# Attention with split key tiles: two float32r products for three, and one column of low parts summed beside TensorE

## The chip, the core and the metric

The kernel runs on one NeuronCore of a Trainium2 chip. The metric is the device time of one execution in microseconds. The kernel before took 1837.95 us in the median of three runs (1836.01 to 1842.63).

## The reference, cut to what matters

Two layers of a hybrid trunk (1152 tokens of width 1024: 128 context tokens, 1024 latent tokens). Each layer has one input projection, then four groups of heads side by side, then one output projection. Two of the groups are softmax attention and are what the change touches:

```
s = einsum('bqhgd,bkhd->bhgqk', qblk, k) * scale
p = softmax(s, axis=-1)
o = einsum('bhgqk,bkhd->bqhgd', p, v)          # float32 throughout
...
o_a = o_a * silu(ggate)                        # group A: 4 query heads on 2 key/value heads, dim 64
o_c = o_c * silu(mgate)                        # group C: 4 latent-attention heads, dim 96, values 64
o   = concat([o_a, o_b, o_c, o_d]) @ w_out
```

Context tokens read only the 128 context keys; latent tokens read 1280 keys (256 cached, 1024 latent). Groups B (gated linear attention) and D (a state-space scan) are chunked scans over the same tokens.

## The kernel before, in words

Everything is float32 in DRAM. Where TensorE multiplies in float32r, the operand is split into a high part (float32r) and a low part (value minus high part), and the product is the sum of the products of the parts; where it multiplies in plain float32, one instruction of the program leaves two matmul records in the trace.

Attention stands in `attend` (line 1093). There are 8 heads a layer, one after the other: four of group A, four of group C. A head has three query blocks (QBLK): block 0 with 128 queries and one key tile, blocks 1 and 2 with 512 queries and ten key tiles of 128 keys each. For one key tile j TensorE makes the scores transposed (keys on partitions, queries along the row) in a PSUM tile `st` (tag B, two buffers), by two (group A) or three (group C) float32r products (line 1102); ScalarE (ACT) takes their exponential; TensorE multiplies by the values into the PSUM tile `po` (tag C, one buffer), rows 0 to 63 the output, row 64 the sum of the weights (the values carry a column of ones).

The weights times values come in two kinds, by the number of the tile:

- even j: the exponential `P` stays float32, and one float32 product with `v` follows (lines 1117 and 1118);
- odd j ("split tiles"): ACT writes the exponential once as float32r (`Ph`, line 1107) and once more in place in float32 (line 1108), VectorE (DVE) subtracts (`Pl`, line 1110), and three float32r products follow: values high by Ph (1112), values low by Ph (1113), values high by Pl (1114). `v_parts` (1148) makes the parts of the values once a head.

At the end of a block ACT copies row 64 to `den` (1127) and rows 0 to 63 to `Ou` (1129); only then may the next block write `po`. For an odd head the sums go through DRAM and come back as reciprocals spread over 64 partitions (`R`), and GpSimd (POOL) multiplies them in (`gt`, line 1144), behind a DMA.

While attention runs, other work is in the same queues: the scans of groups B and D (lines 872 to 1061), for the next head the copies of queries and keys and a maximum over the scores (`maxima`, lines 755 and 756: a product on TensorE and a reduction on DVE), the splitting of the output weights (1085, 1086), and at the end the first tiles of the output projection. The order on each engine is not written out: a scheduler lays the program out in time by a model of its own and fixes each engine's queue; every engine then works its queue in order. So a change of one instruction moves others.

The kernel has one place already where ACT scales a tile by a column and POOL adds it to a sum, with one buffer between them (lines 173 and 174, in the modulation of the layers):

```
pr = wpool.tile([128, 512], F32, name="pr", tag="pr", bufs=1)
act.activation(out=pr, in_=st, func=AF.Identity, scale=c)
pool.tensor_tensor(out=acc[:, r, :], in0=acc[:, r, :], in1=pr, op=ALU.add)
```

Of the kernel before, what the change touches and what calls it, by code (L numbers as in the profile page):

```python
# [8 lines left out]
F32 = mybir.dt.float32  # L9
# [25 lines left out]
def hybrid_trunk_kernel(ctx: ExitStack, tc: tile.TileContext, a):  # L35
# [50 lines left out]
    mask = tri.bitcast(I32)  # L86
    gcum = const.tile([128, 2, 131], F32, name="gcum")
# [291 lines left out]
    for l in range(L):  # L379
# [466 lines left out]
        with ExitStack() as sta:  # L846
# [246 lines left out]
            def attend(h, spasses, scale, v, vi, vh, vl, gate_rows, kd, st):  # L1093

                for b, (q0, nq, kts) in enumerate(QBLK):
                    qs = slice(q0, q0 + nq)
                    po = psC("po")
                    for j, kt in enumerate(kts):
# [5 lines left out]
                        if j % 2:  # L1104

                            Ph = at.tile([128, 512], F32R, name="Ph", tag="Ph", bufs=3)
                            act.activation(out=Ph[:, 0:nq], in_=sp_[:, 0:nq], func=AF.Exp, scale=scale)  # L1107
                            anchors["act"] = act.activation(out=sp_[:, 0:nq], in_=sp_[:, 0:nq], func=AF.Exp, scale=scale)  # L1108
                            Pl = at.tile([128, 512], F32R, name="Pl", tag="Pl", bufs=2)
                            anchors["dve"] = dve.tensor_tensor(out=Pl[:, 0:nq], in0=sp_[:, 0:nq], in1=Ph[:, 0:nq], op=ALU.subtract)  # L1110
                            k = j // 2
                            pe.matmul(po[0:65, 0:nq], lhsT=vh[:, k, :], rhs=Ph[:, 0:nq], start=False, stop=False, skip_group_check=True)
                            pe.matmul(po[0:64, 0:nq], lhsT=vl[:, k, :], rhs=Ph[:, 0:nq], start=False, stop=False, skip_group_check=True)
                            pe.matmul(po[0:65, 0:nq], lhsT=vh[:, k, :], rhs=Pl[:, 0:nq], start=False, stop=last, skip_group_check=True)  # L1114
                        else:
                            P = at.tile([128, 512], F32, name="P", tag="P", bufs=5)
                            anchors["act"] = act.activation(out=P[:, 0:nq], in_=sp_[:, 0:nq], func=AF.Exp, scale=scale)  # L1117
                            pe.matmul(po[0:65, 0:nq], lhsT=v[:, kt, vi, :], rhs=P[:, 0:nq], start=(j == 0), stop=last,  # L1118
                                      skip_group_check=True)
# [6 lines left out]
                    den = nrm.tile([1, 512], F32, name="den", tag="den", bufs=1)  # L1126
# [21 lines left out]
            def v_parts(v, i):  # L1148

                vh = at.tile([128, 5, 65], F32R, name="vh", tag="vh", bufs=2)  # L1150
                vl = at.tile([128, 5, 64], F32R, name="vl", tag="vl", bufs=2)
                act.copy(vh, v[:, 2:KT:2, i, :])
                yield
                pool.tensor_tensor(out=vl, in0=v[:, 2:KT:2, i, 0:64], in1=vh[:, :, 0:64], op=ALU.subtract)
                yield
                return vh, vl

            def prep_mla(h):
# [3 lines left out]
                if h == 0:  # L1162
                    wu = at.tile([128, 512], F32, name="wu", tag="P", bufs=5)
# [63 lines left out]
            def run_mla(h):  # L1227
# [3 lines left out]
                vh, vl = yield from v_parts(state["vm"], i)  # L1231
                yield attend(h, [(KA[i][0:96], QB[i][0:96]), (KA[i], QA[i]), (KB[i], QB[i])], 96.0 ** -0.5, state["vm"], i, vh, vl,
# [248 lines left out]
```

## Time and profile before

| | |
|---|---|
| median of 3 runs | 1837.95 us |
| the profiled execution | 1836.28 us, of which 1834.5 us are the span of the trace |
| attention of layer 0, about | 423 to 870 us of the span |
| attention of layer 1, about | 1300 to 1745 us |
| key tiles of 128 keys by 512 queries | 320: 160 split, 160 in float32 |
| block ends with 512 queries | 32 (2 layers, 8 heads, 2 blocks) |

The span runs from the first to the last instruction. The rows of the trace that the working uses stand in a section below, in numbered groups. In them PE is TensorE's matmuls, PEld its weight loads, DVE VectorE, ACT ScalarE, POOL GpSimd. Matmuls overlap in the pipeline and their ends are modelled, so what one costs in a stream is read from the distance of starts and not from its duration.

### The profile page before, as it was taken

To read this page: it belongs to the slowest core of one execution; us is meant where nothing else is said; L and a number is where in the kernel's file an instruction comes from. 1 tells how busy PE (TensorE), PEld (TensorE's weight loads), DVE (VectorE), ACT (ScalarE), POOL (GpSimd) and SP (SyncE) were. 2 spreads that over 40 slices of the span, in tenths; PEclk is the share of its full clock that TensorE was granted. 3 is DMA by queue.
4 is the path that set the end of the run, shared out by engine and by line. 5 is a ranking of instruction groups with operands and counts; after the bars stand their busy time and mean duration, and the time that the engine had idled before them with its cause. 6 is when DMAs were issued, how large, how long until landed. Compare 5 with 4: busy or idle time off the path is not lost.

```text
span 1834.5 us, 25155 instructions
## 1 busy us (share of the span) xinstructions
PE 1718.5 (94%) x8200; PEld 1312.8 (72%) x8200; DVE 1177.2 (64%) x2297; ACT 859.9 (47%) x1907; POOL 729.2 (40%) x909
## 2 busy tenths in 40 slices
PE   8999998998998998999999999999999899899998
PEld 2787977896665666656887999889666666565676
DVE  5738887647877886772453447543776788678223
ACT  4634422434654765673442162132465467567322
POOL 3633149824343543330343323871434354333011
PEclk9999988999989999999999999999998999999999
DMA  8435353413323321142433333231442332114243
GB/s 296 138 117 156 113 168 103 129 63 119 115 77 85 90 79 47 41 144 86 138 129 104 102 94 91 60 102 37 122 116 76 81 88 83 50 36 149 87 137 115
DMA packets 179684, 190.99 MB, mean 104 GB/s; under 512 B 29406, under 2 KB 140720, under 8 KB 179552
## 3 DMA queue, kind: packets, MB, share of 16 engines
q1 hardware_dynamic: 174208, 179.11, 32.1%
q10 hardware_dynamic: 5344, 10.26, 1.7%
q8 instruction: 65, 1.06, 0.3%
q14 instruction: 67, 0.55, 0.1%
HBM read 141.00 MB, written 48.30 MB: 103 GB/s over the span
## 4 chain that ended last, share of the span: by engine, by line
PE 54%; DVE 17%; DMA 11%; POOL 7%; issue 5%; ACT 4%; SPq 1%; ACTq 0%; POOLq 0%; DVEq 0%
PE psP L267 19%; PE op L267 8%; PE st L1102 5%; PE po L1118 5%; DMA ast<-in_w_ada_dram 2%; PE mx L755 2%; DMA wst<-in_w_in_dram 2%; DVE mx L756 2%; DVE Pl L1110 2%; PE po L1114 1%; DVE acc L176 1%; DMA R<-d_rec 1%; POOL wlo L261 1%; DVE d_DT L1023 1%; PE go L931 1%
## 5 line engine op out<-in xcount | busy, mean ns | idle before, releaser
L756 DVE TENSOR_REDUCE mx<-mx 128x1 f32<-128x512 f32 (+2 forms) x400 | 224.6, 582 | 92.2 <-PE mx L755 90.6
L267 PE MATMUL psP<-whi,hh 128*128 128x512 f32 (+2 forms) x576 | 202.6, 363 | 6.1 <-DVE whi L257 3.7
L267 PE MATMUL psP<-wlo,hh 128*128 128x512 f32 (+2 forms) x576 | 202.8, 361 | 2.1 <-POOL wlo L261 1.9
L267 PE MATMUL psP<-whi,hl 128*128 128x512 f32 (+2 forms) x576 | 187.5, 359 | 0.1
L261 POOL TENSOR_TENSOR wlo<-wst,whi 128x512 fp32r<-128x512 f32 (+3 forms) x106 | 130.6, 1240 | 137.9 <-DVE whi L257 79.0
L267 PE MATMUL psP<-hh,whi 128*128 128x384 f32 x480 | 163.1, 340 | 4.7 <-DVE whi L257 3.8
L1102 PE MATMUL st<-QA,KA 128*128 128x512 f32 (+1 forms) x336 | 164.0, 488 | 0.6 <-DVE Pl L1110 0.4
L267 PE MATMUL psP<-hl,whi 128*128 128x384 f32 x480 | 160.2, 336 | 0.0
L267 PE MATMUL psP<-hh,wlo 128*128 128x384 f32 x480 | 155.0, 337 | 0.1
L1110 DVE TENSOR_TENSOR Pl<-st,Ph 128x512 fp32r<-128x512 f32 x160 | 109.7, 686 | 65.9 <-ACT st L1108 64.2
L1107 ACT ACTIVATE Ph<-st 128x512 fp32r<-128x512 f32 x160 | 95.5, 597 | 107.5 <-PE st L1102 99.1
L1117 ACT ACTIVATE P<-st 128x512 f32<-128x512 f32 (+1 forms) x176 | 99.8, 567 | 79.1 <-PE st L1102 67.1
L1102 PE MATMUL st<-QB,KB 66*128 66x512 f32 (+3 forms) x336 | 133.0, 401 | 0.0
L267 PEld LDWEIGHTS psP<-whi,hh 128*128 128x128 f32 x576 | 110.3, 193 | 20.3 <-DVE whi L257 5.2
L267 PEld LDWEIGHTS psP<-wlo,hh 128*128 128x128 f32 x576 | 110.4, 193 | 17.9 <-POOL wlo L261 5.3
L267 PEld LDWEIGHTS psP<-whi,hl 128*128 128x128 f32 x576 | 108.5, 192 | 12.4 <-DVE hl L226 0.3
L1102 PEld LDWEIGHTS st<-QA,KA 128*128 128x128 f32 x336 | 65.4, 195 | 49.8 <-issue 39.3
L267 PEld LDWEIGHTS psP<-hh,whi 128*128 128x128 f32 x480 | 90.1, 188 | 12.0 <-DVE whi L257 5.5
L1102 PE MATMUL st<-QB,KA 96*128 96x512 f32 (+1 forms) x168 | 93.2, 555 | 2.1 <-ACT P L1117 1.8
L1108 ACT ACTIVATE st<-st 128x512 f32<-128x512 f32 x160 | 94.8, 592 | 0.0
L1118 PE MATMUL po<-P,vm 128*65 128x512 f32 (+1 forms) x176 | 88.7, 586 | 5.9 <-ACT P L1117 3.4
L1144 POOL TENSOR_TENSOR gt<-gt,R 128x512 f32<-128x512 f32 (+1 forms) x24 | 26.6, 1106 | 166.0 <-DMA R<-d_rec 162.3
(369 smaller groups left out, 4325.2 us busy)
## 6 DMA issues: line engine op xcount, KB each, us to landing
ast<-in_w_ada_dram SPq DMA_DIRECT2D x96, 256.0 KB
wst<-in_w_in_dram SPq DMA_DIRECT2D x64, 256.0 KB
wost<-in_w_out_dram SPq DMA_DIRECT2D x16, 512.0 KB
d_xs<-d_xb SPq DMA_DIRECT2D x32, 192.0 KB
ot<-d_oT SPq DMA_DIRECT2D x18, 320.0 KB
d_tok<-vv SPq DMA_DIRECT2D x18, 256.0 KB
d_gt<-gg SPq DMA_DIRECT2D x24, 192.0 KB
g_qk<-d_qk SPq DMA_DIRECT2D x36, 128.0 KB
```

Of the source, the lines that this page charges most:

```text
L176: dve.scalar_tensor_tensor(out=acc[:, r, :], in0=st, scalar=c, in1=acc[:, r, :], op0=ALU.mult, op1=ALU.add)
L261: eng.tensor_tensor(out=lo[:, 0:n], in0=st[:, 0:n], in1=hi[:, 0:n], op=ALU.subtract)
L267: pe.matmul(p, lhsT=lt, rhs=rh, start=(first and i == 0), stop=(last and i == n - 1))
L755: pe.matmul(p[:, 0:n], lhsT=lt_m[:, s], rhs=rh_m[:, o:o + n], start=True, stop=True)
L756: dve.tensor_reduce(out=mx[:, t, i:i + 1], in_=p[:, 0:n], axis=AX.X, op=ALU.max)
L1102: anchors["pe"] = pe.matmul(sp_[:, 0:nq], lhsT=kx[:, ks], rhs=qx[:, qs], start=(i == 0), stop=(i == len(spasses) - 1))
L1107: act.activation(out=Ph[:, 0:nq], in_=sp_[:, 0:nq], func=AF.Exp, scale=scale)
L1108: anchors["act"] = act.activation(out=sp_[:, 0:nq], in_=sp_[:, 0:nq], func=AF.Exp, scale=scale)
L1110: anchors["dve"] = dve.tensor_tensor(out=Pl[:, 0:nq], in0=sp_[:, 0:nq], in1=Ph[:, 0:nq], op=ALU.subtract)
L1117: anchors["act"] = act.activation(out=P[:, 0:nq], in_=sp_[:, 0:nq], func=AF.Exp, scale=scale)
L1118: pe.matmul(po[0:65, 0:nq], lhsT=v[:, kt, vi, :], rhs=P[:, 0:nq], start=(j == 0), stop=last, skip_group_check=True)
L1144: pool.tensor_tensor(out=g[:, 0:nq], in0=g[:, 0:nq], in1=R[:, 0:nq], op=ALU.mult)
```

## The change

In blocks 1 and 2 the split tiles are now the even ones (j = 0, 2, 4, 6, 8), so a block begins with a split tile and ends with a float32 one; block 0 has a float32 tile, as before. A split tile has two products instead of three: `vs` holds in one 128-column operand the high parts of the 64 values and the column of ones (columns 0 to 64) and the low parts of values 1 to 63 (columns 65 to 127). The first product, by Ph, uses all 128 columns, the second, by Pl, the first 65. What has no room is the low part of value 0 (`v0`): ACT multiplies Ph by that column (`acc` for the first split tile, `T0` for the four others), POOL adds the T0 to `acc` (the fourth addition goes to `accr` in float32r), and when the block ends one product with a column of ones (`oner`) adds the sum over the keys to row 0 of `po`.

At the end of a block ACT copies rows 64 to 127 of `po` (the sum of the weights and the low parts) to `lo`, and DVE adds them to rows 0 to 63 into `Ou`, with row 0 of `lo` masked by the column `nz`; so DVE's instruction takes the place of ACT's second copy. P has four buffers instead of five; T0, acc, accr and lo have one each.

```
-                        if j % 2:
+                        if b and j % 2 == 0:
...
                             k = j // 2
-                            pe.matmul(po[0:65, 0:nq], lhsT=vh[:, k, :], rhs=Ph[:, 0:nq], start=False, stop=False, skip_group_check=True)
-                            pe.matmul(po[0:64, 0:nq], lhsT=vl[:, k, :], rhs=Ph[:, 0:nq], start=False, stop=False, skip_group_check=True)
-                            pe.matmul(po[0:65, 0:nq], lhsT=vh[:, k, :], rhs=Pl[:, 0:nq], start=False, stop=last, skip_group_check=True)
+                            c = v0[:, k:k + 1]
+                            if k == 0:
+                                acc = at.tile([128, 512], F32, name="acc", tag="acc", bufs=1)
+                                act.activation(out=acc, in_=Ph, func=AF.Identity, scale=c)
+                            else:
+                                T0 = at.tile([128, 512], F32, name="T0", tag="T0", bufs=1)
+                                act.activation(out=T0, in_=Ph, func=AF.Identity, scale=c)
+                                to = acc if k < 4 else at.tile([128, 512], F32R, name="accr", tag="accr", bufs=1)
+                                anchors["pool"] = pool.tensor_tensor(out=to, in0=acc, in1=T0, op=ALU.add)
+                            pe.matmul(po, lhsT=vs[:, k, :], rhs=Ph, start=(j == 0), stop=False, skip_group_check=True)
+                            pe.matmul(po[0:65, :], lhsT=vs[:, k, 0:65], rhs=Pl, start=False, stop=False, skip_group_check=True)
...
+                    if b:
+                        pe.matmul(po[0:1, :], lhsT=oner, rhs=to, start=False, stop=True, skip_group_check=True)
...
-                    act.copy(den[:, 0:nq], po[64:65, 0:nq])
-                    sp.dma_start(out=d_den[kd, i, qs], in_=den[:, 0:nq])
-                    act.copy(O[64 * i:64 * i + 64, 0:nq], po[0:64, 0:nq])
+                    act.copy(lo[64 * i:64 * i + n, 0:nq], po[64:64 + n, 0:nq])
+                    sp.dma_start(out=d_den[kd, i, qs], in_=lo[64 * i:64 * i + 1, 0:nq])
+                    if b:
+                        dve.scalar_tensor_tensor(out=O[r, :], in0=lo[r, :], scalar=nz[r, :], in1=po[0:64, :], op0=ALU.mult, op1=ALU.add)
+                    else:
+                        act.copy(O[r, 0:nq], po[0:64, 0:nq])
...
-                vh = at.tile([128, 5, 65], F32R, name="vh", tag="vh", bufs=2)
-                vl = at.tile([128, 5, 64], F32R, name="vl", tag="vl", bufs=2)
-                act.copy(vh, v[:, 2:KT:2, i, :])
+                vs = at.tile([128, 5, 128], F32R, name="vs", tag="vs", bufs=2)
+                v0 = at.tile([128, 5], F32, name="v0", tag="v0", bufs=2)
+                x = v[:, 1:KT:2, i, :]
+                act.copy(vs[:, :, 0:65], x)
```

What the scheduler makes of it is shown at three places. First TensorE in layer 0, at the end of a 512-query block of head 5: `st` are scores of the next block, `mx` and `mT` belong to the maximum for the next head. Before:

```order
L1118 MATMUL po<-P,vm 65x512
L1102 MATMUL st<-QB_4250,KA_4247 128x128
L1102 MATMUL st<-QA_4249,KA_4247 128x128
L1102 MATMUL st<-QB_4250,KB_4248 128x128
L772 MATMUL mT<-identr,m 2x128 x4
L755 MATMUL mx<-KA_4247,QB_4250 128x512
L1112 MATMUL po<-Ph,vh 65x512
L1113 MATMUL po<-Ph,vl 64x512
L1114 MATMUL po<-Pl,vh 65x512
```

After:

```order
L1128 MATMUL po<-Ph,vs 128x512
L1129 MATMUL po<-Pl,vs 65x512
L1108 MATMUL st<-QB_4256,KA_4253 128x128
L1108 MATMUL st<-QA_4255,KA_4253 128x128
L1108 MATMUL st<-QB_4256,KB_4254 128x128
L778 MATMUL mT<-identr,m 2x128 x4
L761 MATMUL mx<-KA_4253,QB_4256 128x512
L1133 MATMUL po<-P,vm 65x512
L1138 MATMUL po<-accr,oner 1x512
```

The split tile's products moved to the front of the stretch, and the block is closed by the product with `oner`, which waits for POOL. Second ACT in layer 0, at the seam of heads 6 and 7 (`woh`, `wohl`: output weights; `ohl`, `oQA`: operands of the output projection). Before:

```order
L1127 COPY den<-po 1x512
L1129 COPY Ou_8561<-po 64x512
L1117 ACTIVATE P<-st 128x512
L1107 ACTIVATE Ph<-st 128x512
L1108 ACTIVATE st<-st 128x512
L1285 CAST ohl<-ot 128x640
L1127 COPY den<-po 1x128
L1129 COPY Ou_8226<-po 64x128
L1117 ACTIVATE P<-st 128x512
L1107 ACTIVATE Ph<-st 128x512
L1108 ACTIVATE st<-st 128x512
```

After:

```order
L1147 COPY lo<-po 64x512
L1113 ACTIVATE Ph<-st 128x512
L1114 ACTIVATE st<-st 128x512
L1132 ACTIVATE P<-st 128x512
L1122 ACTIVATE acc<-Ph,v_8693 128x512
L1147 COPY lo<-po 1x128
L1152 COPY Ou_8369<-po 64x128
L1113 ACTIVATE Ph<-st 128x512
L1091 CAST wohl<-wost 128x1024
L1114 ACTIVATE st<-st 128x512
L1125 ACTIVATE T_8805<-Ph,v_8693 128x512
```

One copy of 64x512 went, and an `acc` or a `T` (the tile T0) stands in the queue for each split tile. Third POOL, the end of attention in layer 0 (`wol`, `wohl`, `wo`: low parts of output weights; `gn`: gate rows; `gt`: the product with R). Before:

```order
L1086 TENSOR_TENSOR wol_7760<-wost,woh_7759 128x1024
L1154 TENSOR_TENSOR vl<-vm,vh 128x320
L1086 TENSOR_TENSOR wohl<-wost,wohl 128x1024
L1086 TENSOR_TENSOR wo_8580<-wost,wo_8579 128x1024
L1318 TENSOR_TENSOR gn_8919<-gn_8919,npst 128x1024
L1144 TENSOR_TENSOR gt<-gt,R 128x128
L1144 TENSOR_TENSOR gt<-gt,R 128x512
```

After:

```order
L1127 TENSOR_TENSOR accr<-acc,T_8713 128x512
L1092 TENSOR_TENSOR wol_7880<-wost,woh_7879 128x1024
L1344 TENSOR_TENSOR gn_9107<-gn_9107,npst 128x1024
L1092 TENSOR_TENSOR wohl<-wost,wohl 128x1024
L1127 TENSOR_TENSOR acc<-acc,T_8805 128x512
L1127 TENSOR_TENSOR acc<-acc,T_8826 128x512
L1092 TENSOR_TENSOR wo_8746<-wost,wo_8745 128x1024
L1167 TENSOR_TENSOR gt<-gt,R 128x128
L1127 TENSOR_TENSOR acc<-acc,T_8847 128x512
L1127 TENSOR_TENSOR accr<-acc,T_8868 128x512
L1167 TENSOR_TENSOR gt<-gt,R 128x512
L1127 TENSOR_TENSOR acc<-acc,T_8930 128x512
```

The additions of T0 now share POOL's queue with that work, and stand in front of and behind each `gt`.

## Rows read from the trace of the kernel before

**Rows 1.** The page's line on engines: busy us, share of the span, instructions.
```profile
PE 1718.5 (94%) x8200; PEld 1312.8 (72%) x8200; DVE 1177.2 (64%) x2297; ACT 859.9 (47%) x1907; POOL 729.2 (40%) x909
```
**Rows 2.** Windows: attention of both layers; us, busy of PE, PEld, DVE, ACT, POOL, clock, DMA.
```profile
423.00:870.00 447.00, 411.33 (x1801) 275.27 (x1801) 328.70 (x716) 264.88 (x563) 170.14 (x203) 0.97 0.30 90
1300.00:1745.00 445.00, 410.73 (x1793) 275.18 (x1792) 320.76 (x707) 262.19 (x558) 168.28 (x199) 0.96 0.30 90
```
**Rows 3.** Chain of waits: the page's shares by engine, then each attention stretch by line.
```profile
PE 54%; DVE 17%; DMA 11%; POOL 7%; issue 5%; ACT 4%; SPq 1%; ACTq 0%; POOLq 0%; DVEq 0%
...
by line: PE st L1102 10.1%; PE po L1118 9.0%; DVE mx L756 5.1%; issue 3.8%; PE mx L755 3.5%; DVE Pl L1110 3.0%; PE po L1114 2.9%; DVE d_DT L1023 2.6%; PE op L267 2.4%; PE go L931 2.1%; DMA R<-d_rec 2.1%; PE po L1113 2.1%; PE po L1112 2.0%; 
...
by line: PE st L1102 10.9%; PE po L1118 9.6%; PE mx L755 3.9%; issue 3.6%; DVE mx L756 3.5%; DVE Pl L1110 3.2%; PE po L1114 2.9%; DMA R<-d_rec 2.8%; PE go L931 2.5%; PE op L267 2.5%; DVE d_DT L1023 2.2%; PE po L1113 2.1%; PE att L910 2.1%; 
```
**Rows 4.** Groups by form, products of split tiles: count, busy us, mean ns, idle before.
```profile
L1112 PE MATMUL po<-Ph,vh 128*65 128x512 f32 x160 | 75.9, 474 | 0.5 <-ACT Ph L1107 0.5
L1114 PE MATMUL po<-Pl,vh 128*65 128x512 f32 x160 | 70.3, 440 | 14.8 <-DVE Pl L1110 14.0
...
L1113 PE MATMUL po<-Ph,vl 128*64 128x512 f32 x160 | 64.2, 401 | 0.0
```
**Rows 5.** Timeline of PE in layer 0: start us, duration, what.
```profile
798.29 0.39 PE L1112 MATMUL po<-Ph,vh 128*65 128x512 f32 x1
798.52 0.39 PE L1113 MATMUL po<-Ph,vl 128*64 128x512 f32 x1
798.74 0.39 PE L1114 MATMUL po<-Pl,vh 128*65 128x512 f32 x1
798.97 0.39 PE L1102 MATMUL st<-QB,KA 96*128 96x512 f32 x1
...
799.66 1.02 PE L1118 MATMUL po<-P,vm 128*65 128x512 f32 x2
800.12 0.79 PE L1102 MATMUL st<-QB,KA 96*128 96x512 f32 x1
800.75 0.40 PE L1102 MATMUL st<-QA,KA 128*128 128x512 f32 x1
```
**Rows 6.** Groups by form on ACT: second exponential, scaled tile from SBUF, copy out.
```profile
L1108 ACT ACTIVATE st<-st 128x512 f32<-128x512 f32 x160 | 94.8, 592 | 0.0
...
L173 ACT ACTIVATE pr<-ast,cc 128x512 f32<-128x512 f32 x28 | 20.3, 725 | 33.9 <-POOL acc L174 26.3 <-DMA ast<-in_w_ada_dram 7.5
...
L1129 ACT COPY Ou<-po 64x512 f32<-64x512 f32 x32 | 18.5, 579 | 0.8
```
**Rows 7.** Lines 174 and 173: durations min/median/max; what ended ACT's idle time (us, times).
```profile
L174 POOL TENSOR_TENSOR acc<-acc,pr x28: 1262/1291/1746, 112.6 to 382.4; 128x512 f32<-128x512 f32 x28
...
  POOL acc L174: 26.3, 14
```
**Rows 8.** What ended PE's idle time before lines 1118 and 1114 (us, times).
```profile
  ACT Ou L1129: 16.8, 20
  ACT P L1117: 10.8, 16
...
  DVE Pl L1110: 40.5, 44
```
**Rows 9.** DVE: durations min/median/max by line, and the same lines as groups.
```profile
L1110 DVE TENSOR_TENSOR Pl<-st,Ph x160: 669/691/693, 432.0 to 1747.1; 128x512 fp32r<-128x512 f32 x160
...
L1033 DVE TENSOR_TENSOR d_D<-d_D,d_DT x18: 679/692/1543, 456.0 to 1639.0; 128x512 f32<-128x512 f32 x18
...
L894 DVE TENSOR_TENSOR g_kq<-g_qk,g_Ei x36: 273/287/1377, 443.5 to 1577.4; 128x128 f32<-128x128 f32 x36
...
L894 DVE TENSOR_TENSOR g_kq<-g_qk,g_Ei 128x128 f32<-128x128 f32 x36 | 18.7, 520 | 0.0
...
L1033 DVE TENSOR_TENSOR d_D<-d_D,d_DT 128x512 f32<-128x512 f32 x18 | 17.9, 996 | 2.3 <-ACT d_D L1027 1.7
```
**Rows 10.** Timeline of POOL: one `gt` with the idle time before it.
```profile
853.20 1.97 POOL L1144 TENSOR_TENSOR gt<-gt,R 128x512 f32<-128x512 f32 x1 [25.73 <-DMA R<-d_rec]
```

More of the change, by code (lines that the diff above doesn't have):

```diff
@@ L86, in hybrid_trunk_kernel @@
     mask = tri.bitcast(I32)
+    oner = const.tile([128, 1], F32R, name="oner")
+    nz = const.tile([128, 1], F32, name="nz")
+    pool.memset(nz, 1.0)
+    dve.tensor_copy(oner, nz)
+    for i in range(2):
+        pool.memset(nz[64 * i:64 * i + 1, :], 0.0)
     gcum = const.tile([128, 2, 131], F32, name="gcum")
@@ L1111, in attend @@
                             k = j // 2
-                            pe.matmul(po[0:65, 0:nq], lhsT=vh[:, k, :], rhs=Ph[:, 0:nq], start=False, stop=False, skip_group_check=True)
-                            pe.matmul(po[0:64, 0:nq], lhsT=vl[:, k, :], rhs=Ph[:, 0:nq], start=False, stop=False, skip_group_check=True)
-                            pe.matmul(po[0:65, 0:nq], lhsT=vh[:, k, :], rhs=Pl[:, 0:nq], start=False, stop=last, skip_group_check=True)
+                            c = v0[:, k:k + 1]
[9 more added lines that the diff above has]
+                            pe.matmul(po[0:65, :], lhsT=vs[:, k, 0:65], rhs=Pl, start=False, stop=False, skip_group_check=True)
                         else:
-                            P = at.tile([128, 512], F32, name="P", tag="P", bufs=5)
+                            P = at.tile([128, 512], F32, name="P", tag="P", bufs=4)
                             anchors["act"] = act.activation(out=P[:, 0:nq], in_=sp_[:, 0:nq], func=AF.Exp, scale=scale)
-                            pe.matmul(po[0:65, 0:nq], lhsT=v[:, kt, vi, :], rhs=P[:, 0:nq], start=(j == 0), stop=last,
+                            pe.matmul(po[0:65, 0:nq], lhsT=v[:, kt, vi, :], rhs=P[:, 0:nq], start=(j == 0), stop=(last and not b),
                                       skip_group_check=True)
@@ L1125, in attend @@
                     i = h % 2
-                    den = nrm.tile([1, 512], F32, name="den", tag="den", bufs=1)
-                    act.copy(den[:, 0:nq], po[64:65, 0:nq])
-                    sp.dma_start(out=d_den[kd, i, qs], in_=den[:, 0:nq])
-                    act.copy(O[64 * i:64 * i + 64, 0:nq], po[0:64, 0:nq])
+                    r = slice(64 * i, 64 * i + 64)
+                    lo = nrm.tile([128, 512], F32, name="lo", tag="lo", bufs=1)
+                    n = 64 if b else 1
+                    act.copy(lo[64 * i:64 * i + n, 0:nq], po[64:64 + n, 0:nq])
[4 more added lines that the diff above has]
+                        act.copy(O[r, 0:nq], po[0:64, 0:nq])
                     if i:
@@ L1162, in prep_mla @@
                 if h == 0:
-                    wu = at.tile([128, 512], F32, name="wu", tag="P", bufs=5)
+                    wu = at.tile([128, 512], F32, name="wu", tag="P", bufs=4)
                     wuhl = lp.tile([128, 2, TOK], F32R, name="wuhl", tag="qT")
@@ L1230, in run_mla @@
                     state["st"] = {}
-                vh, vl = yield from v_parts(state["vm"], i)
-                yield attend(h, [(KA[i][0:96], QB[i][0:96]), (KA[i], QA[i]), (KB[i], QB[i])], 96.0 ** -0.5, state["vm"], i, vh, vl,
+                vs, v0 = yield from v_parts(state["vm"], i)
+                yield attend(h, [(KA[i][0:96], QB[i][0:96]), (KA[i], QA[i]), (KB[i], QB[i])], 96.0 ** -0.5, state["vm"], i, vs, v0,
                              d_gt[2 + pr], 6 + pr, state["st"])
```

7 lines of the change are left out of this document (4 added, 3 removed).

## The prediction

> **What bounds the kernel now.** I read the page's line on engines first: TensorE is busy 94% of the span, the next engine, DVE, 64% [rows 1]. Then the windows of the two attention stretches, where all of the change lies: of 447 and 445 us PE is busy in 411 each, DVE in 329 and 321, ACT in 265 and 262, POOL in 170 and 168, and the granted clock is 0.97 and 0.96, so nearly always the upper level of 2.4 GHz [rows 2]. Third the chain of waits. Over the kernel PE holds 54% of it, DVE 17%, POOL 7%, ACT 4%. Inside the attention stretches the scores and the products with the values lead, with DVE's maxima and its Pl between them [rows 3]. So PE is the first bound, but not alone: about half of the path is hand-overs to DVE, ACT, POOL and DMA.
>
> What a product costs is read from starts in a dense piece. The three products of a split tile and the scores behind them start 0.22 to 0.23 us apart, whether they have 64, 65 or 128 columns; I use 0.231 us. The float32 product and one score product lie between 799.66 and 800.75: 1.09 less 0.23 is 0.86 us for the float32 one [rows 5].
>
> **What the change takes from PE.** 160 products of line 1113 go [rows 4]: 160 x 0.231 = 37.0 us. The wider first product has 128 columns like the scores, which stand at the same distance, so it costs no more. 32 products with `oner` come, 512 columns each: 32 x 0.231 = 7.4 us. Swapping even for odd tiles changes no count. PE's own work falls by 29.6 us.
>
> How much of it reaches the end is bounded from two sides. Were PE the only limit, all 29.6 us would come. By the chain of the order as it stands, line 1113 holds 2.1% of 447 and of 445 us [rows 3], that is 18.7 of its 37.0 us, a half; so 15.0 us of the 29.6. The order is laid out anew around the shorter tiles, which speaks for more than the half; the waits on DVE remain, which speaks for less than all. I take the middle, 22 us.
>
> **What it adds, on which engine.**
>
> *ACT.* 160 scaled copies of Ph (128 `T0`, 32 `acc`), the same form as line 173: 0.725 us each, 116 us. The copy of `Ou` goes at 32 block ends (32 x 0.579 = 18.5 us); the copy to `lo` stands where `den` was [rows 6]. ACT gains 97 us over both stretches, from 59% to 70% busy, so it keeps room: 365 us of idle time now. But the queue is in order, and behind each T0 stands an exponential, and behind that PE. Exponentials that come late end 10.8 us of PE's idle time today [rows 8]. I charge 3 us for their growth; the bounds are nothing and 116 us.
>
> *POOL.* 128 additions at 1.29 us (1.75 at worst) [rows 7], 165 us or more, from 38% to 56% busy. None of them is waited for except the fourth of each block, which the closing product needs. From Ph's exponential to that product the way is the second exponential 0.59, T0 0.725, the addition 1.29: 2.6 us [rows 6, 7]. In the new order PE has between 7 and 31 products between the last Ph product and the closing one, one of them in float32. Seven are 6 x 0.231 + 0.86 = 2.25 us, nine are 2.7 us, and six of the 32 ends have nine or fewer. So the wait is mostly covered where POOL is free when T0 is done. I charge 0.1 us for each of 32, 3 us; at worst T0 and the addition lie bare at each end, 32 x 2.0 = 64 us, at best nothing.
>
> *Block ends.* The two copies, 1.16 us, become a copy and a DVE instruction from PSUM and SBUF, 0.58 + 0.69 (priced as Pl, line 1110 [rows 9]), 1.27 us, with one more hand-over, and DVE may be inside another instruction. Behind DVE's instruction stand Pl and the maxima; waiting for it is the first product of the next block. That wait is 16.8 us today, over 20 ends [rows 8]. A tenth more time and, DVE being busy three quarters of the time, a quarter of a microsecond of queue at a third of the ends: 3 us. Bounds: none, and a full DVE instruction at each end, 22 us.
>
> *DVE beside POOL.* An instruction with two operands in SBUF is slower when POOL works: line 1033 takes 0.68 us at least and 1.54 at most, line 894 from 0.27 to 1.38, while Pl, with one operand in PSUM, stays between 0.67 and 0.69 [rows 9]. The two lines lose 18 x (0.996 - 0.679) + 36 x (0.520 - 0.273) = 14.6 us over both layers. POOL will be half again as busy; with as much again for the other instructions of the kind that is some 14 us more DVE time, of which DVE's share of the chain, 17% [rows 3], is 2 us. Bounds: none and 14 us.
>
> The Trainium skill (SBUF — State Buffer, "Who interferes with whom") says that a DVE instruction with two SBUF inputs contends with a GpSimd instruction that reads SBUF, and one with at most one SBUF input outside the two-port modes does not. Lines 1033, 894 and 1110 behave so. It speaks against the change: were all that contention on the path, the sum below would lose 12 us more and come out at no gain.
>
> *The rest.* `v_parts` has one small POOL instruction more, 12 in all, a head ahead of its use and off the path. P loses one buffer of five; tiles pile up where a block ends, which is charged above, so I charge nothing more. If four are too few, it shows as PE idle before scores.
>
> **The sum.** -22 + 3 + 3 + 3 + 2 = -11 us. The profiled execution took 1836.3 us (span 1834.5 and 1.8 around it), 1.7 us under the median of the runs. So 1825 on its scale, 1827 on that of the median; I say **1826 us**. Half a percent, about what a measurement of this kernel can tell from no change, is 9 us: faster means under 1829, slower over 1847.
>
> **The rivals.**
>
> *A, slower: T0's one buffer ties ACT to POOL.* ACT may not write the next T0 before POOL has added the last, and while it stands there no exponential runs. The kernel has this pattern already, lines 173 and 174: at 14 of 28 instructions ACT's idle time was ended by POOL, 26.3 us in all, 1.88 us each [rows 7]. POOL's queue is in order too and can itself stand: before `gt` it sat 25.7 us waiting for R [rows 10], and additions now stand behind each `gt`. If a fifth of the 128 T0 wait 1.88 us, ACT is held 48 us; the 59% in which it is not idle pass on 28 us, and -11 becomes +17: **1853 us**. It breaks even at 11 us passed on, under 0.09 us for each T0, and is slower by half a percent from 0.16 us on. For it: the pattern waited in half of its cases. Against: a T0 comes once in 447 / 80 = 5.6 us, two and a half times what T0 and the addition take together, and the order shown puts P's exponential ahead of `acc`. Chance 0.25.
>
> *B, no change: hidden anyway.* Only the chain's half comes, 15 us, and the 11 us of costs stand against it: **1832 us**. For it: DVE, the second engine, is busy 73% of the stretches and gets more work, and 40.5 us of PE's idle time end on Pl [rows 8], which no edit shortens. Against: the order is made anew. Chance 0.23. The Trainium skill (Perfetto Trace Analysis, "Identifying the Most-Contended Engine") says that TensorE's matmul busy share is no measure of headroom and to take the share of weight loads. Here that is 275 of 447 us, 62% [rows 2]; by that measure 18 of the 29.6 us would come through, and with the same costs the time is 1829, the upper edge of this rival.
>
> *C, faster still: PE is the whole limit.* 27 to 30 us come and the new waits fall into idle time: **1809 us**. For it: PE's 92% in the stretches. Against: the half by the chain. Chance 0.10.
>
> **How the numbers follow.** The forecast has 0.42, its own range 1817 to 1832; A 0.25, B 0.23, C 0.10. The range over the cases runs from C's 1808 to A's 1853. Below 1829 lie C and most of the forecast, 0.47; from 1829 to 1847 B and the rest of the forecast, 0.28; above it A, 0.25.
>
> **What would show it.** In the profile after, products of split tiles number 320 and `oner` 32, starts still 0.23 us apart; PE's busy time in a stretch falls by about 14 us and the stretch by 5 or 6. PE's idle time before the `oner` product stays under 5 us in all, and ACT's idle time ended by the POOL additions under 20 us. Lines 1033 and 894 get slower in the mean. The prediction is wrong if ACT waits for POOL before T0 by 40 us or more (A), if PE's work falls and its idle time grows by as much (B), or if a 128-column product of Ph stands further from its successor than 0.23 us.

## The result, and the profile after

The changed kernel takes 1909.31 us (1906.55 to 1920.64) beside 1837.09 us for the kernel before (1836.01 to 1842.63, now four runs): a ratio of 1.0394, interval 1.0370 to 1.0417, **slower by 72 us**. The forecast was 1826 us, range 1808 to 1853; it is wrong in sign and range. The profiled execution took 1908.6 us.

The page's line on engines, answering to [rows 1]:

```profile
PE 1733.1 (91%) x8072; PEld 1317.7 (69%) x8072; DVE 1287.4 (68%) x2330; ACT 943.3 (49%) x2035; POOL 903.8 (47%) x1052
```

The windows of the two attention stretches from their first score to their last product, columns as in [rows 2]; the kernel before first, then the changed kernel:

```profile
423.20:878.60 455.40, 419.73 (x1839) 281.64 (x1839) 330.51 (x719) 267.87 (x570) 172.51 (x207) 0.97 0.30 90
1296.20:1752.40 456.20, 421.71 (x1838) 282.44 (x1837) 325.69 (x718) 267.66 (x569) 172.74 (x206) 0.96 0.31 91
```

```profile
425.50:907.00 481.50, 426.41 (x1778) 283.87 (x1778) 374.08 (x734) 310.17 (x635) 258.80 (x277) 0.93 0.30 84
1332.00:1826.00 494.00, 429.67 (x1773) 285.94 (x1772) 379.82 (x733) 309.75 (x634) 256.58 (x275) 0.92 0.28 82
```

The stretches grew from 455 to 481 us and from 456 to 494: some 64 of the 72 us. ACT's 42 us and POOL's 86 us more in layer 0 are about what was added. DVE's 44 us are not: 11.8 of them are the new instruction at block ends (23.7 us over both layers), the rest are old instructions that became longer.

The lines of the changed kernel that answer to [rows 4, 6, 7 and 9], by form: count, busy us, mean ns, idle time before and what ended it. 1128 and 1129 are the products by Ph and by Pl, 1125 T0, 1127 POOL's additions, 1138 the closing product, 1150 DVE's `Ou`, 1116 Pl, 1039 and 900 the old lines 1033 and 894, 1029 and 1030 the old 1023 and 1024:

```profile
L1128 PE MATMUL po<-Ph,vs 128*128 128x512 f32 x160 | 83.9, 525 | 9.6 <-ACT Ph L1113 7.9 <-ACT Ou L1152 1.0 <-DVE Ou L1150 0.7
L1129 PE MATMUL po<-Pl,vs 128*65 128x512 f32 x160 | 71.3, 446 | 34.2 <-DVE Pl L1116 33.7
L1138 PE MATMUL po<-accr,oner 128*1 128x512 f32 x32 | 16.6, 520 | 0.6 <-POOL accr L1127 0.6
L1125 ACT ACTIVATE T<-Ph,v 128x512 f32<-128x512 f32 x128 | 92.0, 719 | 14.9 <-POOL acc L1127 14.0
L1127 POOL TENSOR_TENSOR acc<-acc,T 128x512 f32<-128x512 f32 x96 | 126.1, 1314 | 103.6 <-ACT T L1125 103.1
L1150 DVE SCALAR_TENSOR_TENSOR Ou<-lo,nz,po 64x512 f32<-64x512 f32 x32 | 23.7, 740 | 16.8 <-ACT lo L1147 16.4
L1116 DVE TENSOR_TENSOR Pl<-st,Ph 128x512 fp32r<-128x512 f32 x160 | 109.2, 683 | 61.1 <-ACT st L1114 60.3
L1039 DVE TENSOR_TENSOR d_D<-d_D,d_DT 128x512 f32<-128x512 f32 x18 | 20.9, 1160 | 3.0 <-ACT d_D L1033 2.9
L900 DVE TENSOR_TENSOR g_kq<-g_qk,g_Ei 128x128 f32<-128x128 f32 x36 | 22.1, 614 | 0.0
L1029 DVE TENSOR_SCALAR d_DT<-tri,dtv 128x128 f32<-128x128 f32 x72 | 38.5, 610 | 0.1
L1030 DVE SCALAR_TENSOR_TENSOR d_DT<-tri,dtv,d_DT 128x128 f32<-128x128 f32 x72 | 38.1, 574 | 0.0
```

Two of these lines in the kernel before, which the prediction did not read:

```profile
L1024 DVE SCALAR_TENSOR_TENSOR d_DT<-tri,dtv,d_DT 128x128 f32<-128x128 f32 x72 | 28.1, 433 | 0.2
L1023 DVE TENSOR_SCALAR d_DT<-tri,dtv 128x128 f32<-128x128 f32 x72 | 25.0, 424 | 0.2
```

What the reader is to see: the waits that the prediction feared are small. ACT was held by POOL 14.0 us, PE before the closing product 0.6 us. But PE's idle time before the product by Pl went from 14.8 us [rows 4] to 34.2, and Pl itself is no longer than before, 683 ns. The longer DVE instructions are a part of that only: without the sum the wait is 27.7 us already (e1, below). Over all lines PE's idle time that DVE ended grew from 75 to 127 us (the view of waits, summed), with 93 in e1. Two places show how such a wait comes about. The timelines of DVE, POOL and PE in the changed kernel (start us, duration, what, idle time before):

```profile
733.14 2.33 DVE L1030 SCALAR_TENSOR_TENSOR d_DT<-tri,dtv,d_DT 128x128 f32<-128x128 f32 x4
735.40 0.68 DVE L1116 TENSOR_TENSOR Pl<-st,Ph 128x512 fp32r<-128x512 f32 x1
...
733.22 0.58 POOL L1167 TENSOR_TENSOR gt<-gt,R 128x128 f32<-128x128 f32 x1 [2.26 <-DMA R<-d_rec]
733.78 1.29 POOL L1127 TENSOR_TENSOR acc<-acc,T 128x512 f32<-128x512 f32 x1
...
736.13 0.44 PE L1129 MATMUL po<-Pl,vs 128*65 128x512 f32 x1 [3.02 <-DVE Pl L1116]
```

```profile
1338.71 3.86 DVE L1029 TENSOR_SCALAR d_DT<-tri,dtv 128x128 f32<-128x128 f32 x4
1342.49 1.86 DVE L1030 SCALAR_TENSOR_TENSOR d_DT<-tri,dtv,d_DT 128x128 f32<-128x128 f32 x4
1344.28 0.68 DVE L1116 TENSOR_TENSOR Pl<-st,Ph 128x512 fp32r<-128x512 f32 x1
...
1338.63 1.07 POOL L1019 TENSOR_TENSOR d_R<-avh,tri 128x512 fp32r<-128x512 f32 x1
1339.66 1.04 POOL L1019 TENSOR_TENSOR d_R<-avl,tri 128x512 fp32r<-128x512 f32 x1
...
1341.23 1.26 POOL L1127 TENSOR_TENSOR acc<-acc,T 128x512 f32<-128x512 f32 x1
...
1345.01 0.69 PE L1129 MATMUL po<-Pl,vs 128*65 128x512 f32 x1 [5.47 <-DVE Pl L1116]
1345.50 0.63 PE L1108 MATMUL st<-QA,KA 128*128 128x512 f32 x1
1345.92 0.63 PE L1108 MATMUL st<-QB,KB 66*128 66x512 f32 x1
```

At 733.14 four instructions of line 1030 take 2.33 us while POOL is at `gt` and the addition; the median of that line is 0.342 each. Pl waits behind them and PE behind Pl, 3.02 us. At 1338.71 eight take 5.6 us beside POOL's scan work and an addition, and PE stands 5.47. This second place is for the most part an old one: in the kernel before the same eight took 4.3 us, beside the scan and with no addition near:

```profile
1301.46 1.05 DVE L1023 TENSOR_SCALAR d_DT<-tri,dtv 128x128 f32<-128x128 f32 x4
1302.29 3.51 DVE L1024 SCALAR_TENSOR_TENSOR d_DT<-tri,dtv,d_DT 128x128 f32<-128x128 f32 x4
```

The scores behind PE's wait are 0.42 us apart, not 0.23 [rows 5]. The windows around that wait, columns as in [rows 2], tell why:

```profile
1334.00:1339.00 5.00, 3.81 (x16) 1.92 (x15) 4.62 (x8) 4.85 (x11) 4.07 (x9) 1.00 0.47 155
1345.00:1348.00 3.00, 2.99 (x6) 1.53 (x6) 0.91 (x5) 1.09 (x2) 0.00 (x0) 0.50 0.22 73
```

The granted clock is 1.00 before the wait and 0.50 after it, the lower level of 1.2 GHz, though PE is busy all the time. So this wait costs more than its length; the mean clock of the stretches fell from 0.97 and 0.96 [rows 2] to 0.93 and 0.92.

PE's work did fall. Summing for each product the usual distance to the end of its predecessor (30th percentile of its kind) gives about 388 us in each stretch before and 374 after, 13 and 14 us less; it is an estimate, whose level shifts by some us with how kinds are told apart, the difference by half a us. What is not work grew by 39 and 52 us. Of that 19 and 30 us are idle time (window less PE's busy time: 35.7 to 55.1 and 34.5 to 64.3); the rest is in the main work done at the lower clock. By the trace's clock records the lower level held for 31 us of the first stretch before and 65 after, for 34 and 75 of the second.

### The profile page after: what moved, and what is told of

Same layout as the page of the kernel before. It is cut to its first block, busy times and chain, and to the rows that moved or that the text cites. A ratio compares the mean times of both kernels' runs of the same rounds, so it can differ in the third digit from the quotient of the medians.

```text
span 1906.8 us, 25220 instructions
## 1 busy us (share of the span) xinstructions
PE 1733.1 (91%) x8072; PEld 1317.7 (69%) x8072; DVE 1287.4 (68%) x2330; ACT 943.3 (49%) x2035; POOL 903.8 (47%) x1052
## 5 line engine op out<-in xcount | busy, mean ns | idle before, releaser
L1127 POOL TENSOR_TENSOR acc<-acc,T 128x512 f32<-128x512 f32 x96 | 126.1, 1314 | 103.6 <-ACT T L1125 103.1
L1108 PE MATMUL st<-QA,KA 128*128 128x512 f32 (+1 forms) x336 | 168.9, 503 | 3.9 <-ACT P L1132 2.0
L1108 PE MATMUL st<-QB,KB 66*128 66x512 f32 (+3 forms) x336 | 139.2, 418 | 0.0
L1129 PE MATMUL po<-Pl,vs 128*65 128x512 f32 x160 | 71.3, 446 | 34.2 <-DVE Pl L1116 33.7
L1125 ACT ACTIVATE T<-Ph,v 128x512 f32<-128x512 f32 x128 | 92.0, 719 | 14.9 <-POOL acc L1127 14.0
L1108 PE MATMUL st<-QB,KA 96*128 96x512 f32 (+1 forms) x168 | 97.1, 578 | 2.2 <-ACT P L1132 2.2
```

Source lines behind the costliest of these rows:

```text
L1108: anchors["pe"] = pe.matmul(sp_[:, 0:nq], lhsT=kx[:, ks], rhs=qx[:, qs], start=(i == 0), stop=(i == len(spasses) - 1))
L1125: act.activation(out=T0, in_=Ph, func=AF.Identity, scale=c)
L1127: anchors["pool"] = pool.tensor_tensor(out=to, in0=acc, in1=T0, op=ALU.add)
L1129: pe.matmul(po[0:65, :], lhsT=vs[:, k, 0:65], rhs=Pl, start=False, stop=False, skip_group_check=True)
```

## The experiments

All ratios are to the kernel before on the same chip, whose median lay between 1833 and 1847 us from chip to chip; 1% is 18 us. A caution holds for all of them: each edit makes the scheduler lay out every queue anew. Runs that change little but an order differ from their base by 0.5 to 1.0% (e5, e12, e17, e11) and, with the even tiles, by 3% and more (e6, e10).

**Which part costs: the sum, on ACT, on POOL, on DVE.** e1 takes the sum out of the changed kernel, e2 leaves ACT's part, e3 POOL's, e4 gives it to DVE.

```
e1:  - c = v0[...]; acc/T0 (act.activation), pool.tensor_tensor; pe.matmul(po[0:1, :], lhsT=oner, ...)
e2:  - pool.tensor_tensor(out=to, in0=acc, in1=T0)     (T0 of the last tile is written to accr)
e3:  as e1, and  + pool.tensor_tensor(out=acc, in0=acc or the first Ph, in1=Ph)     (k > 0)
e4:  + dve.scalar_tensor_tensor(out=to, in0=Ph, scalar=c, in1=acc, op0=mult, op1=add), no T0; k == 0: dve.tensor_scalar
```

> The changed kernel without the sum for value 0: no scaled copies (acc, T0) on ACT, no additions on POOL, no product with oner. It leaves out the low part of value 0; two products a split tile, even split tiles, the addition of the low parts by DVE at block ends and four P buffers stay. Theory S (the sum costs it all, by the load it puts on ACT and POOL): PE work falls 37 us, the time is 1805 to 1825 us, below the kernel before. Rival E (the new block end, the even order, one P buffer fewer): 1870 to 1900 us. Rival O (the scheduler's new order, whatever the load): anywhere between, with PE's idle time in the two attention stretches still 60 us or more above the kernel before.

> The changed kernel with ACT's 160 scaled copies and the product with oner, but without POOL's additions (the product takes the last scaled copy alone, so the sum holds one tile of five). Theory S, POOL's half (additions slow DVE's instructions beside them by 77 us, and those are what PE waits for): 1820 to 1845 us, with DVE's lines back at their durations of the kernel before. Theory S, ACT's half (97 us more in ACT's queue make exponentials late): 1880 to 1905 us. Both together: 1845 to 1880 us.

> The changed kernel with 128 POOL additions of the same shape and kind (sums of the Ph tiles, not used), no scaled copies on ACT, no product with oner; it leaves out the low part of value 0. POOL's half of theory S: 1865 to 1900 us, with DVE's other lines as slow as in the changed kernel (about 77 us more than before). ACT's half: 1805 to 1835 us, whatever DVE does. If this run less the one without the sum and the ACT run less the one without the sum add up to the changed kernel's distance, the two halves do not act on each other.

> The changed kernel with the sum made by DVE alone (one scaled tile and four scale-and-add instructions a block, 160 in all, straight from Ph), nothing added on ACT or POOL. If DVE's time is what counts (POOL's half: +77 us on DVE is worth some +90 on the time), 110 us or more of new DVE work with two operands in SBUF costs as much or more: 1880 to 1930 us. If ACT's queue or the waits between ACT and POOL are what counts, 1820 to 1850 us.

Measured: e1 1.0150 (1.0121 to 1.0178), e2 1.0172 (1.0143 to 1.0201), e3 1.0295 (1.0266 to 1.0324), e4 1.0391 (1.0362 to 1.0420). So ACT's 160 copies with the closing product cost 0.2%, 4 us, inside the uncertainty; POOL's additions alone 1.45%, 27 us; both 2.4%, 45 us. On DVE the sum costs as much: 137 us of instructions more there, and PE's idle time before the product by Pl 53.3 us. So work put in DVE's queue ahead of Pl does reach PE. POOL's additions alone act elsewhere. The product by Pl in e1, then in e3:

```profile
L1120 PE MATMUL po<-Pl,vs 128*65 128x512 f32 x160 | 70.4, 440 | 27.7 <-DVE Pl L1116 27.5
L1126 PE MATMUL po<-Pl,vs 128*65 128x512 f32 x160 | 73.1, 457 | 24.4 <-DVE Pl L1116 24.0
```

This wait did not grow. What grew is PE's idle time ended by other DVE instructions (93 to 102 us for all of DVE) and by POOL itself (12 to 24 us, on operands of the scans that POOL makes). And 1.5% of the 3.9 are there without the sum, so neither theory alone was enough.

**Without the sum: the block end, the product, the order.** e8 puts the old block end into e1; e7 only drops the product of line 1113 from the kernel before; e6 only splits the even tiles; e5 only shakes the pacing table, to size what a new order can do.

```
e8:  e1 with act.copy(den <- po[64:65]), act.copy(O <- po[0:64]) in place of lo and DVE's Ou
e7:  before, - pe.matmul(po[0:64, 0:nq], lhsT=vl[:, k, :], rhs=Ph[:, 0:nq], ...)
e6:  before, - if j % 2:    + if b and j % 2 == 0:     (values of the other tiles, start at j == 0)
e5:  before, - STEPS = (13, 19, 13, 25, 22, 20, 19, 0)    + STEPS = (14, 18, 14, 24, 23, 19, 20, 0)
```

> The kernel before with nothing changed but the table that paces the other work through the attention: each of its seven numbers moved by one (14, 18, 14, 24, 23, 19, 20 for 13, 19, 13, 25, 22, 20, 19). Rival O (orders differ widely in how well they fit, and the one before was a good one): 1.0% or more slower than before, 1865 us or more on this scale of 1846. If orders differ little: within 0.5%, 1837 to 1855 us. This sizes what a new order alone can cost.

> The kernel before with the even tiles split in blocks 1 and 2, as in the changed kernel; still three products, five P buffers, two ACT copies at a block's end. Rival E, order half (a block that begins with a split tile makes PE wait for two exponentials and a subtraction just when the last block has drained): 1865 to 1890 us. Theory that the new block end does it: 1837 to 1855 us.

> The kernel before without line 1113, the product of the values' low parts by Ph (the low parts of all values are left out); nothing else is changed, so 37 us of PE work go and nothing is added. If that product bounds the path as the prediction had it, 1809 to 1830 us. If the time between Ph and Pl was covered by that product, PE now waits for Pl by as much and the time stays within 0.5%: 1837 to 1855 us. If the new order alone costs, slower than 1855 us.

> The changed kernel without the sum, and with the block end of the kernel before (ACT copies the row of sums and the 64 output rows; the low parts are not added and so left out). Rival E, block-end half (DVE's instruction stands in a busy queue and holds the one po buffer): 1820 to 1850 us, 25 us or more under the run without the sum. If the block end costs nothing: 1865 to 1880 us.

Measured: e5 1.0051 (1.0032 to 1.0069), e6 **1.0310** (1.0273 to 1.0347), e7 0.9925 (0.9904 to 0.9946), e8 1.0098 (1.0068 to 1.0128). The swap of even and odd tiles, with no work added, costs 57 us. Dropping the product brings 14 us of its 37. Its groups show a part of what is missing, answering to L1114 in [rows 4]:

```profile
L1113 PE MATMUL po<-Pl,vh 128*65 128x512 f32 x160 | 72.2, 451 | 20.8 <-DVE Pl L1110 20.1
```

The wait for Pl grew from 14.0 to 20.1 us, as it would if the dropped product had filled time before it; that is 6 of the 23 us. The block end is worth 0.5% (e1 less e8), no more than a shaken order.

**Why the even order costs.** e10 shakes it as e5 shook the odd one; e11 and e12 take one of its marks each, a split tile at a block's start, a float32 tile at its end.

```
e10:  e6 with the STEPS of e5
e11:  before, + if b and j in (0, 2, 5, 7, 9):
e12:  before, + if b and j in (1, 3, 5, 6, 8):
```

> The kernel before with the even tiles split, and each pacing number moved by one as in the earlier run on the odd order (which moved that one by 0.5%). If the even order is bad in itself: again 2.5 to 3.7% over before. If the run with even tiles alone was an unlucky order of the other work: 0 to 2%.

> The kernel before with tiles 0, 2, 5, 7, 9 split: a block begins and ends with a split tile; three products, old block end (two small copies and subtractions more a head in the splitting of values). If it is the split tile at the start of a block that costs: 2 to 3.5% over before, like the even order. If it is the float32 tile at the end: within 0.7%. If it is neither, but the laying out of the other work by chance, anything.

> The kernel before with tiles 1, 3, 5, 6, 8 split: a block begins and ends with a float32 tile. If the split tile at a block's start costs: within 0.7% of before (two split tiles stand side by side, which may cost a little). If the float32 tile at the end costs: 2 to 3.5% over before.

Measured: e10 1.0371 (1.0347 to 1.0395), e11 1.0102 (1.0076 to 1.0128), e12 1.0062 (1.0042 to 1.0081). The even order is bad again, but neither mark alone makes it so. Then the pacing: the preparation of the next head is let in after each tile, and with the even order it falls behind the other kind of tile. e16 and e17 let it in one tile earlier, e18 does so in the changed kernel.

```
e16 (from e6), e17 (from before), e18 (from the changed kernel):
-  while done < total * (j + 1) / 21:
+  while done < total * (j + 2) / 21:
```

> The kernel before with the even tiles split, and the paced work moved one tile earlier (j + 2 for j + 1 in the pacing), so that it falls behind the same kind of tile as in the kernel before. If the phase of the paced work against the split tiles makes the even order slow: 0 to 1.3% over before. If not: 2.5 to 4% over, as the two runs of the even order.

> The kernel before with its own odd tiles, and the paced work moved one tile earlier. If the phase counts: 2 to 4% slower than before. If not: within 0.8%.

> The changed kernel, whole computation, with the paced work one tile earlier, as in the even run that lost all its 3%. If phase and sum add up: the changed kernel's 3.9% less 3.1%, 0.3 to 1.5% over before, 1849 to 1871 us. If the sum needs the room that the shift gives back: 2.5 to 4%, 1888 us or more. Under 1834 us it would beat both kernels.

Measured: e16 **0.9999** (0.9979 to 1.0020), e17 1.0099 (1.0065 to 1.0134), e18 1.0347 (1.0316 to 1.0379). One window of e6 and of e16, layer 0:

```profile
427.00:906.80 479.80, 428.57 (x1835) 284.89 (x1835) 338.12 (x719) 268.98 (x570) 170.72 (x206) 0.95 0.28 84
```

```profile
423.50:879.60 456.10, 419.68 (x1835) 283.10 (x1835) 333.99 (x719) 269.05 (x570) 169.57 (x206) 0.96 0.31 89
```

The same instructions on every engine, 24 us apart. PE's waits in e6, then in e16 (us in all, times, longest):

```profile
PE po L1114 <- DVE Pl L1110: 15.5, 21, 3.4
PE kT L902 <- DVE g_kq L894: 13.3, 6, 3.4
PE mx L755 <- DVE mx L756: 12.5, 21, 1.8
...
PE st L1102 <- ACT P L1117: 7.2, 12, 1.6
```

```profile
PE po L1114 <- DVE Pl L1110: 19.5, 23, 3.2
PE kT L902 <- DVE g_kq L894: 10.7, 4, 4.8
...
PE mx L755 <- DVE mx L756: 4.4, 11, 0.9
...
PE st L1102 <- ACT P L1117: 3.9, 6, 1.1
```

So the even order is not slow in itself: how the tile kinds fall against the paced work decided. The waits saved are many small ones, on the maxima, the exponentials and the scans; the one for Pl grew. Why this phase suits and the other not, the runs do not tell. Nor does it carry over: in the changed kernel the same shift brought 0.5% of its 3.9, with intervals that overlap, and in the kernel before it cost 1.0%. An order's cost belongs to one program.

**Does the sum cost in the odd order too, and by what?** e9 is the changed kernel with odd tiles, whole computation; e13 takes its sum away; e14 puts only POOL's additions into the kernel before; e15 keeps POOL as long with memsets, which only write.

```
e9:   changed kernel, + if j % 2:   and at j == 0, b > 0:  + pe.matmul(po, lhsT=a row of zeros, rhs=..., start=True)
e13:  e9 without the sum
e14:  before, + pool.tensor_tensor(out=acc, in0=acc or the first Ph, in1=Ph) x128; P bufs=4
e15:  before, + pool.memset(acc[:, 0:n], 0.0) for n in (512, 512, 256) x128; P bufs=4
```

> The changed kernel, whole computation, with the odd tiles split as in the kernel before. So that the 128 rows of po start at zero, each 512-query block begins with one more product (a row of zeros), 32 in all, 7.4 us; the closing product now follows right behind the last split tile. If the even order is what costs (run with even tiles alone: +3.1%): about 50 us less than the changed kernel, 1840 to 1870 us on the scale of 1833. If the sum on ACT and POOL is what costs: 1885 to 1915 us. A bare wait of PE for the last addition (2 us at 32 ends) would show before the product with oner.

> The run of the whole computation in the odd order without its sum: no copies on ACT, no additions, no product with oner (the low part of value 0 is left out). Two products, the addition by DVE at a block's end and the product of zeros at its start stay. If the sum costs in any order: 2 to 4% under that run, 1835 to 1870 us on the scale of 1843. If the sum is dear only where order and sum meet badly: within 1.5% of it.

> The kernel before with 128 POOL additions of Ph tiles (128x512, results unused) and four P buffers, nothing else. If POOL's additions cost by slowing DVE's other lines and standing in POOL's queue, whatever the order: 1 to 2.5% slower than before, with DVE 40 us or more busier. If they cost only in the even order: within 0.7%.

> The kernel before with POOL kept busy in the same 128 places by memsets (512, 512 and 256 columns, together about 1.4 us, as long as an addition) behind the tile's second exponential, and four P buffers. If the additions cost by reading SBUF beside DVE: DVE's time stays within 25 us of before and the time within 0.8%, 1830 to 1860 us. If they cost by standing in POOL's queue: 1.5 to 3% slower, 1870 to 1900 us, with DVE not slower.

Measured: e9 1.0432 (1.0402 to 1.0462), e13 1.0086 (1.0058 to 1.0114), e14 **1.0247** (1.0204 to 1.0291), e15 1.0137 (1.0117 to 1.0157). The sum costs 3.5% in the odd order, and 128 additions (with one buffer fewer for P) 45 us in the kernel before, where nothing waits for them. The expected bare wait before the closing product did not show (0.9 us). The lines on engines, first of e14, then of e15:

```profile
PE 1739.3 (92%) x8200; PEld 1321.1 (70%) x8200; DVE 1251.7 (66%) x2297; ACT 863.0 (46%) x1907; POOL 894.8 (47%) x1037
```

```profile
PE 1731.7 (93%) x8200; PEld 1320.9 (71%) x8200; DVE 1206.3 (65%) x2297; ACT 862.1 (46%) x1907; POOL 900.6 (48%) x1293
```

And groups by form, again e14 first (1120 is its product by Pl):

```profile
L1024 DVE SCALAR_TENSOR_TENSOR d_DT<-tri,dtv,d_DT 128x128 f32<-128x128 f32 x72 | 36.0, 548 | 0.0
L1023 DVE TENSOR_SCALAR d_DT<-tri,dtv 128x128 f32<-128x128 f32 x72 | 34.6, 560 | 0.1
L1120 PE MATMUL po<-Pl,vh 128*65 128x512 f32 x160 | 72.1, 451 | 13.7 <-DVE Pl L1110 12.9
```

```profile
L1023 DVE TENSOR_SCALAR d_DT<-tri,dtv 128x128 f32<-128x128 f32 x72 | 33.6, 596 | 0.2
L1024 DVE SCALAR_TENSOR_TENSOR d_DT<-tri,dtv,d_DT 128x128 f32<-128x128 f32 x72 | 28.8, 443 | 0.0
```

POOL is busy as long in both. DVE, with the same 2297 instructions as before, is 75 us busier with the additions [rows 1] and 29 with the memsets. An order alone moves DVE too: over the kernel before and its eight variants without added work (e5, e6, e7, e10, e11, e12, e16, e17) it is busy 1177 to 1203 us, and the kernel before is the least. So the memsets' 1206.3 hardly stand out, the additions' 1251.7 do. The same holds in three other pairs: 42 us more from e1 to e3, 77 from e1 to the changed kernel, 43 from e13 to e9.

Line 1024, which has two operands in SBUF, is slowed by additions (433 to 548 ns) and not by memsets (443). Over the thirteen runs without the sum or other added POOL work its mean lies between 356 and 433 ns, over the five with additions between 460 and 574. Line 1023, one operand and a column, is long beside both, 560 and 596 ns, but less clearly: without added work it lies between 387 and 544.

The bounds for e15 did not part the theories. 1.4% (1.2 to 1.6) is over "within 0.8%" and at the edge of the "1.5 to 3%" of POOL's queue, while "DVE not slower" failed by 29 us. Shown is that reading additions make DVE 42 to 77 us busier. That they cost 1.1% more time than memsets of the same length, with the same P buffers, rests on one pair of runs and is about what an order can do. How the 1.4% of the memsets divides between POOL's queue, DVE, the buffer and the new order stays open, so more than half of the additions' 2.5% need not have come through DVE. PE's idle time does not settle it: DVE ended 75 us of it before, 85 with memsets, 97 with additions, POOL 4, 13 and 14, but orders alone moved DVE's figure between 68 and 106 (e5, e10). The product by Pl waits 13.7 us in e14, no longer than before.

The Trainium skill (SBUF — State Buffer, "Who interferes with whom") says that a DVE instruction with two SBUF inputs contends with a GpSimd instruction that reads SBUF and not with one that only writes it, and that DVE's two-port modes, which a `tensor_scalar` can enter, contend with GpSimd. Line 1024 agrees with the first (548 and 443 ns); line 1023 would fit the second, within what the orders leave open.

No kernel with the whole computation beat the kernel before: e16 equals it, and e7, which does beat it by 14 us, lacks the low parts of the values.

## Why the prediction was wrong, point by point

- **PE's work**: right in size. 320 split products and 32 closing ones ran, and the work fell by some 13 and 14 us a layer, 14.8 by the sum on record. In dense pieces the 128-column product stands 0.23 to 0.24 us from its successor, so that sign of being wrong did not come. But the sign to look for was wrong: PE's *busy* time did not fall, it rose from 419.7 to 426.4 us in layer 0, since more of it ran at the lower clock (mean 0.97, then 0.93), where a product by Pl lasts some 0.69 us instead of 0.42. Work must be read from the distances in dense pieces at the upper clock.
- **What reaches the end**: "I take the middle, 22 us" of 29.6 was too much. The one clean run, e7, passed on 14 of 37 us; by that, 11 of 29.6. The lower bound (a half) was still too high; the product removed had covered a part of the wait for Pl.
- **"Swapping even for odd tiles changes no count"**: failed. It changes no count, and cost 57 us by itself (e6), though not by its nature (e16). The order was credited with a gain ("the order is made anew") and never bounded from the side of a loss. The sum on record has no term for it. In the changed kernel it cannot be split off: e8, with even tiles, two products and four P buffers, lies 1.7% above e7.
- **"DVE beside POOL ... Bounds: none and 14 us"**: failed. The forecast had some 14 us more DVE time, 2 us of it on the path; additions made DVE 42 to 77 us busier, and by themselves cost 27 us (e3) and 45 us (e14) with nothing waiting for their results. The prediction had priced two lines, 1033 and 894, and guessed "as much again" for the others; lines 1023 and 1024 alone gained 23.5 us in the changed kernel (13.5 and 10.0 by the rows above), nearly four times what those two gained (3.4 and 3.0). It then passed on 17% of that, DVE's share of the chain; but the chain's share of an engine tells what stands on the path now, not what an engine 73% busy does to the path when its queue gets longer. What stands behind the additions in POOL's own queue had no term: PE's idle time that POOL ended was 12 us longer in e3 than in e1. The citation of the Trainium skill had the rule and the direction right, and the size ("12 us more") wrong by the same guess; it also left out the one-operand instructions.
- **ACT, closing product, block ends**, 3 us each: inside their bounds. ACT with the closing product 4 us (e2), the closing product's wait 0.6 us, the block end 9 us (e1 less e8, no more than an order's chance).
- **Two waits read too long**: the 40.5 us on Pl and the 16.8 us on `Ou` [rows 8] count the idle time of the weight loads with that of the matmuls. Of the first 14.0 are the matmuls' [rows 4]; of the second some 6. So "40.5 us of PE's idle time end on Pl" was about three times too much.
- **Rival A** gave the right side by the wrong mechanism: ACT waited for POOL before T0 14 us, not 40 or more, so its own sign says no. **Rival B**'s sign came, idle time growing as PE's work falls, but more than three times as far as the work fell, idle time and slow clock together. **C** fell. The rivals' times are on the scale of the profiled execution and the forecast a us above it; nothing hangs on that.

In the changed kernel's own order the 72 us are thus: 18 with even tiles and two products (e8), 9 for the block end (e1), 45 for the sum, of which POOL's additions alone are 27, ACT's copies alone 4, and 14 come only when both are there. Against the forecast of 11 us less that makes 83 us: 37 for the sum, which was charged 8, 40 for order and products, which were credited with 22, and 6 for the block end. The sum's cost came back in both orders, 2.4% and 3.5%, and its additions' in e3 and e14; its size holds to a per cent or so. The 18 us do not stand clear of what an order can do (e6). That four P buffers cost nothing was not tried alone.

## What to carry to other kernels

Work put on POOL beside a busy DVE is paid in part by DVE, and may be paid by what stands behind it in POOL's own queue: before moving elementwise work to a free POOL, list every DVE line with a wide gap between its least and its mean duration, not two of them, and ask what PE waits for behind them and behind POOL. Where a scheduler lays out all queues, a swap that changes no count still needs a term of its own with a bound on both sides; shake the pacing of the kernel before to size it, more than once: here one shake moved 0.5% and another layout 3%. And an instruction that is removed may have been the cover of a wait (e7 suggests it): look at what follows it in the queue.

## What the runs showed of the hardware that was not expected

One short DVE instruction can last through several POOL instructions. Line 1029 takes 270 ns at least and 3077 at most:

```profile
L1029 DVE TENSOR_SCALAR d_DT<-tri,dtv x72: 270/276/3077, 427.9 to 1705.9; 128x128 f32<-128x128 f32 x72
```

The longest is the second of four, and around it stand on DVE and POOL:

```profile
776.28 4.07 DVE L1029 TENSOR_SCALAR d_DT<-tri,dtv 128x128 f32<-128x128 f32 x4
...
776.83 1.80 POOL L1248 TENSOR_TENSOR KB<-kn,KA 64x352 fp32r<-64x352 f32 x2
778.60 1.26 POOL L1167 TENSOR_TENSOR gt<-gt,R 128x512 f32<-128x512 f32 x1
```

It runs from 776.87 to 779.95, past two `KB` and a `gt`, and ends 0.1 us behind the `gt`. None of the three is an addition: such meetings are in the kernel before too, where the longest of this line took 1649 ns. What the additions change is how many there are: 29 of the 72 instructions of this line last over 0.5 us, 13 before and 8 in e1. The median stays at 276 ns, so the loss sits in a part of the instructions, and a mean from one run says little of a line with few of them: a 128x4 cast (line 768) lay between 236 and 512 ns in runs without added POOL work, and at 268 in e14 with it.

And the wait that follows on PE can cost twice, once as idle time and once at the lower clock behind it, as at 1345 above, where the granted clock was 0.50.
